# State space mixer: three kinds of loads on GpSimd's queue, the factors two quarters ahead

## The chip, the cores and the metric

The kernel runs on one core of a Trainium2 chip. The metric is the device time of one execution in microseconds; the numbers shown are the median of three runs. One execution was also recorded by the hardware profiler; all rows below come from it.

## What is computed

Two transformer blocks of two layers each on a sequence of 512 tokens and 1024 channels, all in float32. The change lies in the second block's second layer, the S5 state space mixer. Its core in the reference:

```python
u = h.reshape(b, seq, 64, 16)                 # 64 groups of 16 channels
mag = exp(lr * dt); ab = mag * (cos(li * dt) + i sin(li * dt))
bb = ((ab - 1) / (lr + i li))[..., None] * b  # 64 states to a group
bu = einsum('gpc,bsgc->bsgp', bb, u)
x = scan(x[t] = ab * x[t-1] + bu[t])          # over the sequence
y = real(einsum('gcp,bsgp->bsgc', c, x)) + d * u
g_a, g_b = split(gelu(y) @ w_glu, 2)
x_out = x_in + g_a * sigmoid(g_b)
```

(written here with complex numbers; the reference keeps real and imaginary parts apart).

## The kernel before

The sequence is cut into 64 steps of 8 tokens. A group then has a vector of 8 x 16 = 128 numbers at each of the 64 steps. Three things are made ahead, in the stage of the first feed-forward layer, and stored in the chip's HBM: `w_d`, the factors that turn 128 inputs into what one step adds to the states; `v_d`, the output factors that turn a state into 128 outputs; `k_d`, the kernels of the Toeplitz matrices, which map the 128 inputs of a step to outputs of the same step; and with them `tab_d`, the turns and decays by which the states are rotated and decayed from step to step.

`mixer3` works in four quarters of 16 groups. I call them 0 to 3. For each quarter q TensorE and VectorE do this:

- `blocks(q)`: 64 small products of the factors w and the inputs U[q] (line 1655), into PSUM.
- `states`: VectorE turns these by `tab` (lines 1671 to 1673), scans them with the decays (1674) and turns them back into X (1677 to 1681).
- `within(q)`: 32 products of U[q] and the Toeplitz matrices tm (line 1701).
- `outputs`: 64 products of X and the output factors v on top of them (line 1712); ScalarE copies the result out (1714).
- `gelus(q)`: eight transposes (1724), gelu on ScalarE, and a split into a high and a low part for the next projection (223, 224).

TensorE's order is written out by hand: blocks(0), within(0), blocks(1), outputs(0), then twice {within(q+1), blocks(q+2), gelus(q), outputs(q+1)}, then within(3), gelus(2), outputs(3) and the projection `w_gl`. All other engines' orders come from a planner, which lays the instructions out by their order in the program and by when it expects them to be ready; a load that needs a slot is placed with a wait for the last reader of the tile that was there.

The loads of the stage: the factors `w5` (1 MB a quarter) and turns `tab` (768 KB) by `s5_load` (lines 1611 to 1620), tm (1 MB, in eight pieces, line 1691) and v (1 MB, line 1693) by `factors`. Factors, tm and v share one tag, w5, with 4 slots; the profile names all three `w` and tells them apart by their source `w_d`, `k_d`, `v_d`. The turns have 2 slots. Factors and turns of quarters 0 and 1 are asked for through GpSimd's queue while the stage before (`ple(0)`, a gated projection with weights `w_pg`) still runs; those of quarters 2 and 3, all tm and all v go through SyncE's queue, each where the program comes to it: tm and v of q+1, then factors and turns of q+2. GpSimd has one computation in `mixer3`, the scaling of U[1] to U[3] (line 1736).

Of the kernel before, what the change touches and what calls it, by code (L numbers as in the profile page):

```python
# [140 lines left out]
def _build(ctx, tc, A, out, dbg, upto, cap):  # L141
    nc = tc.nc
    V, S, G, PE = nc.vector, nc.scalar, nc.gpsimd, nc.tensor

    def pool(stack, name, **kw):
        return stack.enter_context(tc.tile_pool(name=name, bufs=1, reuse_waits="tile", **kw))
# [7 lines left out]
    def tl(p, shape, tag, bufs=1, dt=F32):  # L154
        return p.tile(list(shape), dt, name=tag, tag=tag, bufs=bufs)
# [6 lines left out]
    def ps_(tag="ps", bufs=3):  # L162
        return tl(pp if tag in ("ps", "pm") else phase["px"], [128, T], tag, bufs)
# [1225 lines left out]
    w_d = tl(dp, [128, 32, 2, 128], "w_d")  # L1389
    v_d = tl(dp, [128, 32, 2, 128], "v_d")  # L1390
    tab_d = tl(dp, [128, 3, 32, 64], "tab_d")
# [218 lines left out]

    def s5_load(wq, q):

        if loaded:
            return loaded.pop(0)
        w = tl(wq, [128, 8, 2, 128], "w5", 4)
        e = nc.sync if q > 1 else G
        e.dma_start(w, w_d[:, 8 * q:8 * q + 8])
        tb = tl(wq, [128, 3, 8, 64], "tab", 2)
        e.dma_start(tb, tab_d[:, :, 8 * q:8 * q + 8])
        return w, tb  # L1620

    loaded = []

    def mixer3(U, wq, hp):
        with ExitStack() as st:
# [17 lines left out]
            def blocks(q):  # L1643

                if not q:
                    for h in range(2):
                        o = U[q].rearrange("p (b e) j -> p b e j", b=2)[:, :, 4 * h:4 * h + 4]
                        scaled.append(V.tensor_tensor(o, o, rj[:, None, None, :].to_broadcast([128, 2, 4, 64]), op=MUL).ins)
                w, tb = s5_load(wq, q)
                s = []  # L1650
                for a in range(2):
                    p = ps_("pb", 1) if a and q % 2 else ps_()
                    for e in range(8):
                        for ab in range(2):
                            PE.matmul(p[64 * ab:64 * ab + 64, e * 64:e * 64 + 64], w[:, e, a, 64 * ab:64 * ab + 64],
                                      U[q][:, 8 * ab + e], start=True, stop=True)
                    s.append(p)
                return s, tb

            def states(s, tb, gs=8):  # L1660

                tr, ti, rr = (tb[:, i].rearrange("p g j -> p (g j)") for i in range(3))
                X = tl(bp, [128, 2, 8, 64], "X", 2)
                V.memset(X[:, :, :, 0:1], 0.0)
                b = [tl(bp, [128, T], f"b{a}", 2) for a in range(2)]
                m = [f_() for a in range(2)]
                for g0 in range(0, 8, gs):
                    c, g = slice(g0 * 64, (g0 + gs) * 64), slice(g0, g0 + gs)
                    for a in range(2):
                        o, n = b[a][:, c], m[a][:, c]  # L1670
                        V.tensor_tensor(o, s[a][:, c], tr[:, c], op=MUL)
                        V.tensor_tensor(n, s[1 - a][:, c], ti[:, c], op=MUL)
                        V.tensor_tensor(o, o, n, op=SUB if a else ADD)
                        V.tensor_tensor_scan(o, rr[:, c], o, 0.0, op0=MUL, op1=ADD)
                    v = [y.rearrange("p (g j) -> p g j", g=8)[:, g, :63] for y in b + m]
                    for a in range(2):
                        V.tensor_tensor(X[:, a, g, 1:], v[a], tb[:, 0, g, :63], op=MUL)
                        V.tensor_tensor(v[2 + a], v[a], tb[:, 1, g, :63], op=MUL)
                    for a in range(2):
                        o = X[:, a, g, 1:]  # L1680
                        V.tensor_tensor(o, o, v[3 - a], op=ADD if a else SUB)
                return X
# [3 lines left out]
            def factors(q):  # L1686

                tm = tl(wq, [128, 16, 128], "w5", 4)
                for t in range(8):
                    o = 112 - 16 * t  # L1690
                    nc.sync.dma_start(tm[t:128:8], k_d[16 * q:16 * q + 16, :, o:o + 128].rearrange("g c m -> c g m"))
                v = tl(wq, [128, 8, 2, 128], "w5", 4)
                nc.sync.dma_start(v, v_d[:, 8 * q:8 * q + 8])
                return tm, v

            def within(q, tm):

                ps = [ps_("py", 2) for _ in range(2)]
                for e in range(8):
                    for ab in range(2):  # L1700
                        PE.matmul(ps[e // 4][sides[ab], e % 4 * 128:e % 4 * 128 + 128], U[q][:, 8 * ab + e], tm[:, 8 * ab + e],
                                  start=(e % 4 == 0), stop=False)
                return ps
# [14 lines left out]
            def gelus(q, o):  # L1718
                cs = (2 * q, 2 * q + 1)
                ys = [f_() for _ in cs]  # L1720
                for h in range(2):
                    p = ps_("pm", 2)
                    for t in range(4):
                        PE.transpose(p[:, t * 128:t * 128 + 128], o[:, 4 * h + t].rearrange("p e c -> p (e c)"), ident)
                    for ab, y in enumerate(ys):
                        S.activation(y[:, 256 * h:256 * h + 256].rearrange("p (t j) -> p t j", t=4),
                                     p.rearrange("p (t a j) -> p t a j", t=4, a=2)[:, :, ab], AF.Gelu_apprx_tanh)
                for c, y in zip(cs, ys):
                    if "s5" in dbg:
                        nc.sync.dma_start(dbg["s5"][c], y)  # L1730
                    acts.append(hl(hp, 8, y))

            s0 = blocks(0)
            with tc.issue_after(scaled[-1]):
                for q in range(1, 4):
                    G.tensor_tensor(U[q], U[q], rj[:, None, :].to_broadcast([128, 16, 64]), op=MUL)
            tm, v = factors(0)
            X = states(*s0, gs=4)
            y = within(0, tm)
            s1 = blocks(1)  # L1740
            o = outputs(y, v, X)
            X = states(*s1)
            for q in range(2):
                tm, v = factors(q + 1)
                y = within(q + 1, tm)
                s1 = blocks(q + 2)
                gelus(q, o)
                o = outputs(y, v, X)
                X = states(*s1)
            tm, v = factors(3)  # L1750
            y = within(3, tm)
            gelus(2, o)
# [328 lines left out]
    with ExitStack() as b2:  # L2081
# [8 lines left out]
        with ExitStack() as st:  # L2090
            p = pool(st, "s5u")
            wq = pool(st, "s5w")
# [32 lines left out]
```

## Time and profile before

| | |
|---|---|
| median of three runs | 2476.03 us (2470.3 to 2476.96) |
| profiled execution | 2467.97 us |
| its span | 2466.2 us |
| TensorE busy | 2339.5 us, 95% |
| VectorE busy | 1764.8 us, 72% |
| ScalarE busy | 1090.6 us, 44% |
| GpSimd busy | 518.4 us, 21% |

The span is the time from the first to the last instruction. Times in rows are microseconds from its start. The stage that the change touches lies between 1903 and 1965; the loads for it begin at 1855. In the rows PE is TensorE, DVE VectorE, ACT ScalarE, POOL GpSimd, SPq SyncE's queue.

### The profile page before, as it was taken

The page shows a single profiled execution, that of the slowest core. Times are in us where ns is not written, and L with a number is a line of the kernel's source. Part 1 is how long each engine was busy: PE and PEld are TensorE (multiplying, and loading weights), DVE is VectorE, ACT ScalarE, POOL GpSimd, SP SyncE. Part 2 cuts the span into 40 slices and gives each one's busy share as a digit, 9 for nine tenths or more (in the row PEclk, how much of TensorE's full clock was granted, in tenths as well). Part 3 has the DMA queues.
Part 4 walks back from the last instruction along what each step waited for, and adds up shares of the span by engine and source line. Part 5 has one row for each costly group of instructions (what it writes and reads, how often), then busy time and mean ns, then how long its engine had stood idle before and what let it go on. Part 6 is the DMA issues. An engine that isn't in the chain of part 4 may idle for free.

```text
span 2466.2 us, 35818 instructions
## 1 busy us (share of the span) xinstructions
PE 2339.5 (95%) x13205; PEld 1921.3 (78%) x13206; DVE 1764.8 (72%) x3319; ACT 1090.6 (44%) x1706; POOL 518.4 (21%) x510
## 2 busy tenths in 40 slices
PE   7999899899999998999989999999999899999999
PEld 4767799677777775899766777778787788888887
DVE  6985678699996886667686677737847756745755
ACT  3444588434443434786334434324433234433432
POOL 0001444100000002444110295666520000000000
PEclk9999899899999998999899999999999899999999
DMA  9862699554345222897421233344337632323342
GB/s 347 291 207 82 234 324 331 170 181 128 117 140 180 86 70 100 295 329 251 138 69 61 83 105 119 102 132 123 98 113 239 204 111 94 100 86 106 97 125 94
DMA packets 136790, 385.95 MB, mean 156 GB/s; under 512 B 24696, under 2 KB 41208, under 8 KB 134560
## 3 DMA queue, kind: packets, MB, share of 16 engines
q1 hardware_dynamic: 121408, 338.51, 41.5%
q0 software_dynamic: 7552, 26.74, 3.1%
q10 hardware_dynamic: 7648, 18.32, 2.1%
q8 instruction: 109, 1.79, 0.3%
q14 instruction: 73, 0.60, 0.1%
HBM read 354.13 MB, written 29.38 MB: 156 GB/s over the span
## 4 chain that ended last, share of the span: by engine, by line
PE 43%; DVE 7%; ACT 1%; issue 1%; DMA 0%; ACTq 0%; DVEq 0%
PE ps L268 13%; PE ps L270 13%; PE ps L269 13%; DVE wl L224 1%; DVE hc L2013 1%; ACT wh L223 0%; DMA tab<-tab_d 0%; PE pm L372 0%; PE sk L1587 0%; PE pa L512 0%; PE pm L530 0%; PE ps L1091 0%; PE ps L1092 0%; PE po L538 0%; DVE hc L2017 0%
## 5 line engine op out<-in xcount | busy, mean ns | idle before, releaser
L268 PE MATMUL ps<-hi,wh 128*128 128x512 f32 (+2 forms) x2248 | 898.9, 400 | 3.9 <-ACT hi L485 3.2
L270 PE MATMUL ps<-hi,wl 128*128 128x512 f32 (+2 forms) x2248 | 884.6, 394 | 8.8 <-DVE wl L224 8.8
L269 PE MATMUL ps<-lo,wh 128*128 128x512 f32 (+2 forms) x2248 | 884.5, 394 | 3.1 <-DVE lo L486 2.4
L223 ACT ACTIVATE wh<-w 128x1024 fp32r<-128x1024 f32 (+2 forms) x327 | 310.8, 951 | 572.1 <-PE ps L269 376.6
L224 DVE TENSOR_TENSOR wl<-w,wh 128x1024 fp32r<-128x1024 f32 (+3 forms) x323 | 371.3, 1150 | 211.6 <-ACT wh L223 207.3
L270 PEld LDWEIGHTS ps<-hi,wl 128*128 128x128 f32 (+1 forms) x2248 | 424.4, 189 | 109.2 <-DVE wl L224 13.8
L268 PEld LDWEIGHTS ps<-hi,wh 128*128 128x128 f32 (+1 forms) x2248 | 425.5, 189 | 106.7 <-issue 12.4
L269 PEld LDWEIGHTS ps<-lo,wh 128*128 128x128 f32 (+1 forms) x2248 | 425.2, 189 | 96.2 <-DVE lo L486 4.3
L224 DVE TENSOR_TENSOR wl<-we,wh 128x1024 fp32r<-128x1024 f32 x128 | 169.4, 1336 | 61.1 <-ACT wh L223 59.1
L929 POOL TENSOR_TENSOR hl<-hT,hh 128x1024 fp32r<-128x1024 f32 x60 | 138.4, 2307 | 173.3 <-ACT hh L928 96.0
L2013 DVE SCALAR_TENSOR_TENSOR hc<-f,cols,hc 128x511 f32<-128x511 f32 (+1 forms) x176 | 152.4, 866 | 6.4 <-ACT hc L2011 3.2
L223 ACT ACTIVATE wh<-we 128x1024 fp32r<-128x1024 f32 x128 | 135.3, 1059 | 47.6 <-PE pa L947 23.3
L909 PE MATMUL ps<-ht,w 128*128 128x128 f32 x1024 | 125.9, 276 | 5.2 <-ACT ht L959 5.0
L909 PEld LDWEIGHTS ps<-ht,w 128*128 128x128 f32 x1024 | 119.4, 192 | 7.4 <-ACT ht L959 7.1
L726 POOL IOTA io<- 128x512 f32 x2 | 1.1, 562 | 572.0 <-PE ps L270 415.6
L2009 DVE TENSOR_TENSOR f<-ps,rb 128x512 f32<-128x512 f32 x88 | 60.4, 686 | 71.2 <-PE ps L270 70.9
L441 DVE CUSTOM_DVE_ANT_0 we<-we,crow 128x1024 f32<-128x1024 f32 x80 | 96.3, 1214 | 3.4 <-DMA we<-in_ada_t_dram 3.1
L947 PE MATMUL pa<-wh,hh 128*128 128x256 f32 x496 | 89.2, 301 | 0.0
L223 ACT ACTIVATE hi<-hc 128x512 fp32r<-128x512 f32 x44 | 27.8, 632 | 128.0 <-DVE hc L2017 128.0
L491 DVE SCALAR_TENSOR_TENSOR x<-ps,mod,x 128x512 f32<-128x512 f32 x52 | 38.9, 748 | 59.0 <-PE ps L270 51.5
L947 PE MATMUL pa<-wl,hh 128*128 128x256 f32 x496 | 78.7, 281 | 1.4 <-DVE wl L224 1.4
L947 PE MATMUL pa<-wh,hl 128*128 128x256 f32 x496 | 79.1, 281 | 0.0
(572 smaller groups left out, 3319.1 us busy)
## 6 DMA issues: line engine op xcount, KB each, us to landing
we<-in_w_ex_dram SPq DMA_DIRECT2D x128, 512.0 KB, 5.7
w<-in_w_fu_dram SPq DMA_DIRECT2D x88, 512.0 KB, 3.5
we<-in_ada_t_dram SPq DMA_DIRECT2D x80, 512.0 KB, 5.0
w<-in_w_ex_dram SPq DMA_DIRECT2D x64, 512.0 KB, 5.4
w<-in_w_si_dram SPq DMA_DIRECT2D x48, 512.0 KB, 3.5
w<-in_w_fd_dram SPq DMA_DIRECT2D x32, 512.0 KB, 3.8
w<-in_w_ei_dram SPq DMA_DIRECT2D x20, 512.0 KB, 3.6
aw<-in_ada_w_dram SPq DMA_DIRECT2D x16, 512.0 KB, 10.2
```

The source lines that it names most:

```text
L223: S.activation(hi, src, AF.Copy)
L224: eng.tensor_tensor(lo, src, hi.bitcast(F32), op=SUB)
L268: PE.matmul(ps[:m], a, h, start=(not more and k + j == 0), stop=False)
L269: PE.matmul(ps[:m], a, l, start=False, stop=False)
L270: PE.matmul(ps[:m], b, h, start=False, stop=(last and k + j == nk - 1))
L441: V.tensor_tensor_reduce(w, w, row, 1.0, 0.0, op0=MUL, op1=ADD, accum_out=st[:, n:n + 1])
L491: V.scalar_tensor_tensor(xs[c], ps, mod(l, seg, c), xs[c], op0=MUL, op1=ADD)
L909: PE.matmul(p[:, c * 128:(c + 1) * 128], w2[:, (4 * q + c) * 128:(4 * q + c + 1) * 128], hd, start=True, stop=True)
L929: (V if e < 2 else G).tensor_tensor(hl_, win, hh.bitcast(F32), op=SUB)
L947: PE.matmul(hp[:, 0:256], h[:, 4 * n + k], w[:, k * 256:(k + 1) * 256], start=(n + i + k == 0), stop=(n + i + k == 6))
L2009: V.tensor_tensor(t, next(up)[1], rb, op=MUL)
L2013: V.scalar_tensor_tensor(c[:, d:], t[:, :T - d], C(f"fw{l}{2 - d}", n), c[:, d:], op0=MUL, op1=ADD)
```

## The change

The factors and turns of quarters 2 and 3, and all output factors, go through GpSimd's queue instead of SyncE's. The list `loaded`, in which the first two quarters' loads wait, is now filled in the loop too: factors and turns of q+2 are asked for in the program ahead of the Toeplitz matrices and output factors of q+1, and `blocks` takes them from the list.

```diff
     def s5_load(wq, q):
 
-        if loaded:
-            return loaded.pop(0)
         w = tl(wq, [128, 8, 2, 128], "w5", 4)
-        e = nc.sync if q > 1 else G
-        e.dma_start(w, w_d[:, 8 * q:8 * q + 8])
+        G.dma_start(w, w_d[:, 8 * q:8 * q + 8])
         tb = tl(wq, [128, 3, 8, 64], "tab", 2)
-        e.dma_start(tb, tab_d[:, :, 8 * q:8 * q + 8])
+        G.dma_start(tb, tab_d[:, :, 8 * q:8 * q + 8])
         return w, tb
...
-                w, tb = s5_load(wq, q)
+                w, tb = loaded.pop(0)
...
                 v = tl(wq, [128, 8, 2, 128], "w5", 4)
-                nc.sync.dma_start(v, v_d[:, 8 * q:8 * q + 8])
+                G.dma_start(v, v_d[:, 8 * q:8 * q + 8])
                 return tm, v
...
             for q in range(2):
+                loaded.append(s5_load(wq, q + 2))
                 tm, v = factors(q + 1)
                 y = within(q + 1, tm)
                 s1 = blocks(q + 2)
```

## Rows read from the trace of the kernel before

**Rows 1.** Busy time by stage: window, length, busy us (x instructions) of PE, PEld, DVE, ACT, POOL; clock, DMA share, GB/s
```profile
1903.00:1965.00 62.00, 44.90 (x675) 41.88 (x675) 52.03 (x101) 13.92 (x30) 7.91 (x3) 0.78 0.75 217
1965.00:2466.00 501.00, 496.07 (x2232) 410.84 (x2230) 294.75 (x392) 190.64 (x248) 0.00 (x0) 1.00 0.32 101
```

**Rows 2.** Timeline of TensorE, 1909 to 1966: start, us, line, what [idle before <-releaser]
```profile
1914.92 3.58 PE L1701 MATMUL py<-w,U 128*64 128x128 f32 x32
...
1929.70 3.06 PE L1701 MATMUL py<-w,U 128*64 128x128 f32 x32
1932.59 2.03 PE L1655 MATMUL ps<-U,w 128*64 128x64 f32 x64
...
1939.47 1.97 PE L1701 MATMUL py<-w,U 128*64 128x128 f32 x32 [0.19 <-ACT o L1714]
1944.65 1.20 PE L1655 MATMUL ps<-U,w 128*64 128x64 f32 x32 [3.21 <-DMA w<-w_d]
1945.61 1.96 PE L1655 MATMUL pb<-U,w 128*64 128x64 f32 x32
...
1949.25 3.71 PE L1712 MATMUL py<-w,X 64*64 64x128 f32 x64
...
1959.34 5.32 PE L1712 MATMUL py<-w,X 64*64 64x128 f32 x64 [2.69 <-DVE X L1681]
```

**Rows 3.** Timeline of VectorE, 1934 to 1961
```profile
1934.16 1.26 DVE L1681 TENSOR_TENSOR X<-X,f 128x504 f32<-128x504 f32 x2
...
1945.49 1.27 DVE L1681 TENSOR_TENSOR X<-X,f 128x504 f32<-128x504 f32 x2
1948.47 0.69 DVE L1671 TENSOR_TENSOR b<-ps,tab 128x512 f32<-128x512 f32 x1 [1.71 <-DMA tab<-tab_d]
```

**Rows 4.** The chain of waits, 1850 to 2010: start, us, what
```profile
1936.97 11.41 DMA tab<-tab_d
```

**Rows 5.** Timeline of SyncE's queue, 1840 to 2010
```profile
1915.18 6.08 SPq L1691 DMA_DIRECT2D w<-k_d  x8
...
1929.81 5.88 SPq L1691 DMA_DIRECT2D w<-k_d  x8
...
1936.42 0.38 SPq L1617 DMA_DIRECT2D w<-w_d  x1
...
1939.32 9.60 SPq L1691 DMA_DIRECT2D w<-k_d  x8
```

**Rows 6.** What SyncE's queue waited for, 1939 to 1950: us, times, longest
```profile
SPq L1691 <- DMA tab<-tab_d: 3.3, 1, 3.3
```

**Rows 7.** DMA issues: transfer, queue, count, size, median us to landing
```profile
v_d<-s_vr POOLq DMA_DIRECT2D x8, 256.0 KB, 2.8
...
w<-w_d POOLq DMA_DIRECT2D x2, 1024.0 KB, 8.7
...
tab<-tab_d POOLq DMA_DIRECT2D x2, 768.0 KB, 11.4
```

**Rows 8.** Line 1691, pieces of tm1, of tm2, of tm3 (each eight): us to landing
```profile
DMA to landing us min/median/max: 3.0/3.2/3.9
...
DMA to landing us min/median/max: 3.9/4.1/4.9
...
DMA to landing us min/median/max: 4.9/9.4/9.4
```

**Rows 9.** Timeline of GpSimd, 1780 to 2010
```profile
1908.87 7.91 POOL L1736 TENSOR_TENSOR U<-U,rj 128x1024 f32<-128x1024 f32 x3 [51.47 <-DVE rj L1639]
```

**Rows 10.** Timelines of VectorE and TensorE, the fourth column of the projection before
```profile
1872.59 1.23 DVE L224 TENSOR_TENSOR wl<-w,wh 128x1024 fp32r<-128x1024 f32 x1 [2.81 <-ACT wh L223]
...
1874.79 0.39 PE L270 MATMUL ps<-hi,wl 128*128 128x512 f32 x1
```

**Rows 11.** Busy time by stretch, columns as in rows 1
```profile
1940.00:1945.00 5.00, 1.79 (x38) 1.57 (x35) 5.00 (x9) 0.00 (x0) 0.00 (x0) 1.00 0.99 392
```

**Rows 12.** Line 1648: durations ns min/median/max, first and last start
```profile
L1648 DVE TENSOR_TENSOR U<-U,rj x2: 691/1761/2831, 1908.8 to 1909.4; 128x512 f32<-128x512 f32 x2
```

## The prediction

> **What bounds the kernel now.** The windows by stage come first [rows 1]. In the last 501 us, from 1965 on, TensorE is busy for 496.07; a microsecond won or lost before 1965 is therefore handed on to the end almost whole. In the 62 us of the state space stage (1903 to 1965) TensorE is busy for only 44.90 us, VectorE for 52.03. Of such a stretch the waits matter. The timeline of TensorE [rows 2] has two that bear on the change: 3.21 us before 1944.65, ended by the landing of the factors of quarter 3 (`w<-w_d`), and 2.69 us before 1959.34, ended by VectorE's X. VectorE's timeline [rows 3] shows why the first is not the dear one: states(2) ends at 1945.49 + 1.27 = 1946.76 and states(3) starts at 1948.47, after 1.71 us of waiting for `tab<-tab_d`, the turns of quarter 3. The chain of waits agrees: it runs through VectorE's states and has one transfer in it, those turns, 11.41 us from 1936.97 [rows 4]. What can be won here is thus those 1.71 us; TensorE's 3.21 us lie beside VectorE's states(2).
>
> **The change, part by part.** Nothing is computed more or less; eight transfers change their queue or their place (the four output factors, and factors and turns of quarters 2 and 3), and the four slots of tag w5 are handed out in another order. I number the quarters 0 to 3 and call the Toeplitz matrices tm.
>
> *SyncE's queue.* It loses the 2 x 2 factor and turn transfers and the 4 output factors. Today it asks for the factors of 3 at 1936.42, after tm2, whose eight pieces start at 1929.81 and take 5.88 us to ask for [rows 5]. It also pays later: of the eight pieces of tm3 the last ones wait, 3.3 us of it for the turns of 3 to land [rows 6]. These waits go, and the first weights of the next projection are asked for some microseconds sooner. Nobody late waits for either, so I price this at 0.
>
> *Factors of 3.* They go ahead of tm2 and so take the slot that tm2 takes today, the one free just before 1929.81 [rows 5]. Asked at about 1929.9, with 8.7 us to landing as GpSimd's earlier ones [rows 7], they are there by 1938.6. The wait of 3.21 us goes.
>
> *tm2.* It is late next. Its slot is now the one of tm1, which within(1) gives free: 1929.70 + 3.06 = 1932.76 [rows 2], 3 us after today. The last piece starts 5.88 - 0.6 = 5.3 us after the first, at 1938.1. How long a piece takes is bounded by 3.0 us (tm1 today, best) and 9.4 (tm3, behind 2.75 MB in the same queue) [rows 8]; tm2 has the queue to itself now, so I take 4.5, from tm2's own row of 3.9 to 4.9. Landed: 1942.6. Within(2) then starts at 1942.6 and not 1939.47. It took 1.97 us; after such an idle time TensorE ran blocks(3) in 1945.61 + 1.96 - 1944.65 = 2.92 where blocks(2), run without a pause, took 2.03 [rows 2], so I add 0.9: over at 1945.5. The first half of blocks(3) is ready at 1946.5, the second at 1947.5.
>
> *Turns of 3.* Both tab slots stay as they are; this one comes free with states(1), 1934.16 + 1.26 = 1935.42 [rows 3]. Asked at 1935.5 and not 1936.97, and no longer behind the factors and output factors of SyncE's queue. GpSimd's two turn transfers took 11.4 us (median), with 3.5 MB of their own queue around them; stores of GpSimd of a third of the size took 2.8 [rows 7]. Between 2.8 and 11.4 I take 8: 1943.5. At the upper end it is 1946.9, still within 0.2 us of the end of states(2). So states(3) starts with states(2)'s end, and its second operation meets the second half of blocks(3) at 1947.5 with some 0.1 us to wait: 1948.47 - 1946.87 = 1.6 us won. Outputs(3) follows X as today [rows 2, 3].
>
> *tm1 and the output factors of 1.* The factors of 2 take the first free slot; tm1 waits for within(0) to end, 1914.92 + 3.58 = 1918.5, 3.3 us later than 1915.18 [rows 2, 5]. 5.3 and 3.9 us later it has landed: 1927.7, for within(1) at 1929.70. Covered; with 9.4 us it would be 1933.2, and 3.5 us late, of which blocks(2) has 0.8 before VectorE feels it: the loss would be 2.7. The output factors of 1 may stand behind the turns of 2 in GpSimd's queue, which wait for states(0); outputs(1) wait for states(1) anyway, a whole quarter of VectorE's work later. Price 0. Of blocks(2)'s 0.8 us: it ends at 1932.59 + 2.03 = 1934.62 [rows 2], states(1) at 1935.42 [rows 3].
>
> *Output factors of 0.* They have no slot to wait for and GpSimd is idle for the 51.47 us before 1908.87, so from 1857.40 [rows 9], so I expect them at about 1857.4, 1 MB into the busiest stretch of loads. There one load of the projection before has little slack: its half for VectorE is done at 1872.59 + 1.23 = 1873.82 and first used at 1874.79, 1.0 us [rows 10]. At the pace of a full stretch, 392 GB/s [rows 11], 1 MB is 2.7 us; less the slack that bounds the loss by 1.7. The lower end is 0, below it nothing, since that load's queue loses nothing. I take 0.3: they stand last behind 3.5 MB of their own queue and meet that load only at its end. If GpSimd's queue puts them behind the scaling instead (1908.87 + 7.91 = 1916.8), 8.7 us make it 1925.5, and TensorE waits in outputs(0), in a stretch where VectorE has the pace; the 0.8 us of blocks(2) are left as cover there too.
>
> *The waits added to GpSimd's queue.* The scaling of U is its only computation there and stands ahead of them; nobody else waits behind a stuck transfer but the next transfer.
>
> Sum: 1.6 won, 0.3 lost, 1.3 us faster. The profiled execution took 2467.97 us (span 2466.2 and 1.8 around it) and would take 2466.7. It is 8.1 us below the median of the three timed runs, 2476.03, themselves 6.7 apart; the sum is a difference, so I put it on the median: 2474.7 us.
>
> **A rule against it.** In 1940 to 1945 the 16 DMA engines were busy to 0.99 and moved 392 GB/s [rows 11]: full, with all of it in one queue. The Trainium skill, "DMA: Bandwidth & Descriptors", section "Issuing engines are not separate DMA queues", says that transfers from several engines run on the same 16 DMA engines and that a second issuer saves only the time to issue. By the rows alone the sum above counts on order (factors of 3 some 6 us sooner), not on bandwidth; by that rule the turns of 3 would land no sooner than now and the sum would be 0, which is the first rival.
>
> **Rivals.**
> *No change* (0.22). The engines are full, the turns still land at 1948; or the freed SyncE lets the two splits of the next weights (0.68 us each) slip in among VectorE's states(3), +1.4 against 1.6. For it: the share of 0.99. Against: the factors of 3 move out of that stretch. 2476 us.
>
> *tm2 too late* (0.14), the slower side: 9.4 us for its last piece gives 1947.5, within(2) to 1950.4, blocks(3)'s first half at 1951.4, states(3) 3 us later than 1948.47: 2479 us. It decides from 1944.5 for tm2's landing, 2 us after my value. For it: the turns and output factors of GpSimd's queue run at the same time. Against: SyncE's queue holds nothing else.
>
> *GpSimd starved* (0.07). Row: VectorE's product of U took 2831 ns beside GpSimd's scaling, and 691 without [rows 12], so the two hold each other up. VectorE is busy all 5.00 us of 1940 to 1945 [rows 11]. If GpSimd could not put its transfers out until VectorE pauses, the turns of 2 would start at 1935.4 and those of 3 at the next pause; with 6 us to landing each (between the 2.8 and 8.7 of [rows 7]) that is 6 twice less the 1.7 waited for today, some 10 us: 2486. The Trainium skill, "SBUF — State Buffer", section "Who interferes with whom", has a lock of this kind, for some forms of VectorE's instructions. Against: GpSimd's stores landed in 2.8 us (median of eight) while VectorE worked [rows 7].
>
> *More is won* (0.12): outputs(3) took 5.32 us after the idle time, outputs(2), 64 of the same without a pause, 3.71 [rows 2]; with 1.6 us more won: 2473. Against: VectorE still ends last, so TensorE still waits before it.
>
> **How the numbers follow.** My case has 0.45. Within 0.3% (7.4 us, about what a measurement of this kernel can tell from no change) lie all but the starved queue; the runs' own spread moves a tenth of the cases over either bound, more below, as the profiled execution and one run lie well under the median. So 0.11 faster, 0.80 same, 0.09 slower. Range 2467 to 2482: from the winning case less the spread to tm2 too late and the spread. My own case: 2471 to 2478.
>
> **What would show it.** Right: no `tab` wait on VectorE near 1947, none on `w<-w_d` on TensorE, in its place a wait of some 3 us for `w<-k_d` ahead of within(2); GpSimd's first output factors near 1857. Wrong: states(3) starting after 1948.5, a TensorE gap in 1872 to 1876 above 0.5 us, or a GpSimd landing above 12 us.

## The result, and the profile after

The changed kernel takes 2506.71 us (median of six runs, 2496.67 to 2512.41); the kernel before, in the same session, 2476.49 us (2470.3 to 2481.23). The ratio is 1.0107, with a 95% interval of 1.0087 to 1.0127. Forecast were 2474.7 us, and a range that ended at 2482. The forecast was wrong, in sign and by 32 us.

The profiled execution of the changed kernel took 2496.67 us, of which 2494.9 are its span, 28.7 us more than the profiled execution before. The windows by stage of the kernel after (columns as in [rows 1]) say where:

```profile
1910.00:1993.40 83.40, 44.78 (x671) 42.26 (x672) 53.68 (x100) 13.76 (x30) 12.31 (x10) 0.73 0.56 149
1993.40:2494.90 501.50, 496.38 (x2232) 410.97 (x2232) 294.86 (x392) 191.04 (x248) 0.00 (x0) 1.00 0.33 101
```

After the stage nothing changed: 496.38 of 501.50 us busy on TensorE, 496.07 of 501.00 before. In the stage TensorE and VectorE work as long as before (44.78 and 53.68 us; 44.90 and 52.03), in a longer time, and the DMA engines moved 149 GB/s in place of 217. So it is waits. I measure the stage from here on from the product that makes rj (two matmuls into `pm`, just ahead of the scaling of U) to the end of outputs(3): 56.80 us before (1907.86 to 1964.66), 78.65 after (1914.70 to 1993.35), 21.85 more. Of the other 6.9 us, 6.1 stand ahead of the first instruction that was changed (GpSimd's ask for the factors of 0, at 1854.77 before and at 1860.83 after); in the other kernels below, whose work up to there is the same, it falls between 1858 and 1869, so I put this down to the spread between executions. 0.8 lie between that ask and the scaling of U.

The timeline of TensorE after has the waits. Line 1698 is within, 1652 blocks, 1709 outputs; line numbers from `states` on are three lower than before:

```profile
1934.58 3.57 PE L1709 MATMUL py<-w,X 64*64 64x128 f32 x32 [3.18 <-DVE X L1678]
1955.30 3.45 PE L1698 MATMUL py<-w,U 128*64 128x128 f32 x32 [17.15 <-DMA w<-k_d]
...
1971.27 3.68 PE L1698 MATMUL py<-w,U 128*64 128x128 f32 x32 [5.99 <-DMA w<-k_d]
...
1987.97 5.38 PE L1709 MATMUL py<-w,X 64*64 64x128 f32 x64 [3.28 <-DVE X L1678]
```

Within(1) waits for tm1 for 17.15 us; before, it followed at once at 1929.70 [rows 2]. Within(2) waits for tm2 for 5.99 us, before 0.19. The 3.21 us for the factors of 3 are gone, as forecast. VectorE's timeline shows that nothing covers the first wait any more:

```profile
1922.71 2.85 DVE L1670 TENSOR_TENSOR b<-b,f 128x256 f32<-128x256 f32 x1
...
1934.44 1.28 DVE L224 TENSOR_TENSOR wl<-w,wh 128x512 fp32r<-128x512 f32 x2
...
1959.72 0.69 DVE L1668 TENSOR_TENSOR b<-ps,tab 128x512 f32<-128x512 f32 x1 [14.57 <-PE ps L1652]
```

States(2) starts 14.57 us late, as blocks(2) stand behind within(1) in TensorE's order. The wait for `tab` of [rows 3] is gone. In the middle row are two splits of weights of the next projection. Why tm1 is late stands in SyncE's queue (timeline of its asks, after):

```profile
1915.06 20.42 SPq L241 DMA_DIRECT2D w<-in_w_gl_dram  x4
1935.58 9.46 SPq L1688 DMA_DIRECT2D w<-k_d  x8
...
1958.78 12.64 SPq L1688 DMA_DIRECT2D w<-k_d  x16
```

Before, the eight pieces of tm1 went out at 1915.18 [rows 5] and all weights of `w_gl` stood behind tm3, from 1949.66:

```profile
1949.66 56.75 SPq L241 DMA_DIRECT2D w<-in_w_gl_dram  x15
```

After, four weight loads stand ahead of tm1. Counted from the start of the stage, as the two traces are shifted against each other, the first weights are asked for at 0.36 us and not at 41.80, and tm1 at 20.88 and not at 7.32. What the queue waited for between 1930 and 1937 (us, times, longest):

```profile
SPq L241 <- DVE wl L224: 15.8, 1, 15.8
```

The fourth weight load needs a place that VectorE's split of an earlier one gives free. That split is the middle row above and stands behind states(0) in VectorE's order, at 1934.44, so the fourth load goes out at about 1935.2, and tm1, which has had its own place since 1924.9 (the end of within(0)), at 1935.58. It is a queue blocked by the load at its head.

Nor do the pieces land as before. Line 1688, the eight pieces of tm1, and the eight of tm2, us from ask to landing:

```profile
DMA to landing us min/median/max: 12.5/12.6/12.7
...
DMA to landing us min/median/max: 3.0/5.0/7.1
```

Tm1's pieces took 3.0 to 3.9 before [rows 8]. Tm2's late landing in this kernel is first of all a late ask: its slot is tm1's, and it goes out at 1958.78, when within(1) has ended. In 1935 to 1956 GpSimd's queue moved 3.67 MB (turns of 2, v1, factors and turns of 3) and held the engines for 55.1% of the time, SyncE's 1.57 MB and 35.8%. GpSimd's own timeline:

```profile
1863.45 0.56 POOL L1690 DMA_DIRECT2D w<-v_d  x1
1915.71 5.62 POOL L1733 TENSOR_TENSOR U<-U,rj 128x1024 f32<-128x1024 f32 x2 [51.70 <-DVE rj L1636]
1922.30 0.59 POOL L1614 DMA_DIRECT2D w<-w_d  x1 [0.97 <-PE ps L1652]
1922.90 2.36 POOL L1733 TENSOR_TENSOR U<-U,rj 128x1024 f32<-128x1024 f32 x1
...
1938.46 0.53 POOL L1614 DMA_DIRECT2D w<-w_d  x1 [2.94 <-PE py L1709]
1944.22 0.76 POOL L1616 DMA_DIRECT2D tab<-tab_d  x1 [5.23 <-DVE f L1675]
```

V0 is asked for at 1863.45, as early as forecast. The factors of 2 stand ahead of the third scaling of U and wait 0.97 us there for blocks(0), so that this scaling runs beside VectorE's product of 1922.71, which takes 2.85 us and not 1.21.

### The profile page after: what moved, and what is told of

Its sections match the earlier page's. It is cut to its first block, busy times and chain, and to the rows that moved or that the text cites. A ratio compares the mean times of both kernels' runs of the same rounds, so it can differ in the third digit from the quotient of the medians.

```text
span 2494.9 us, 35833 instructions
## 1 busy us (share of the span) xinstructions
PE 2342.3 (94%) x13205; PEld 1923.3 (77%) x13206; DVE 1768.5 (71%) x3319; ACT 1090.2 (44%) x1706; POOL 523.2 (21%) x518
```

## Experiments

Two theories. *Blocked queue*: the loss is made by what the planner put ahead of tm1 in SyncE's queue once that had been emptied. *Shared engines*: GpSimd's megabyte transfers and the Toeplitz pieces use the same 16 DMA engines, and the pieces land late wherever they stand in a queue. Two smaller suspects beside them: the order of factors of 2 and scaling, and v0's early transfer. The expectations name a third theory, *slots*: that the order in which the tag's four slots are handed out costs the time by itself. It wanted 2500 us or more in three kernels that took 2481 to 2485, and is out as the main cause. All runs in one table; each group has its own runs of the kernel before on the same chip (medians, in the order of the rows: 2476.49 for the changed kernel; 2476.18 for the next four; 2474.04 for four; 2476.74 for three; 2476.04 for the last two). The ratio is the one on record, and not the quotient of the two medians:

| kernel | us | ratio to before, 95% | stage, us | longest wait in it |
|---|---|---|---|---|
| before | 2476.49 | | 56.80 | 3.21 factors of 3 |
| changed | 2506.71 | 1.0107 (1.0087 to 1.0127) | 78.65 | 17.15 tm1 |
| weights behind tm3 | 2485.35 | 1.0039 (1.0023 to 1.0054) | 65.24 | 10.92 tm2 |
| changed order, old queues | 2481.33 | 1.0025 (1.0006 to 1.0044) | 62.60 | 9.56 tm1 |
| changed, v on SyncE | 2481.03 | 1.0019 (1.0000 to 1.0038) | 63.18 | 7.46 factors of 3 |
| all on GpSimd, old order | 2485.51 | 1.0030 (1.0011 to 1.0049) | 64.62 | 5.63 factors of 2 |
| weights behind, tm1 held | 2502.64 | 1.0104 (1.0081 to 1.0128) | 82.46 | 19.18 tm1 |
| weights behind, order, v0 on SyncE | 2480.74 | 1.0026 (1.0009 to 1.0043) | 62.23 | 7.78 tm2 |
| before, spare loads | 2485.73 | 1.0042 (1.0025 to 1.0059) | 65.45 | 5.53 factors of 3 |
| before, turns on GpSimd | 2472.77 | 0.9988 (0.9972 to 1.0005) | 54.49 | 2.03 tm2 |
| weights behind, order, v0 on SyncE, small loads | 2476.63 | 0.9997 (0.9980 to 1.0014) | 55.75 | 3.32 tm2 |
| before, v on GpSimd | 2482.04 | 1.0021 (1.0005 to 1.0037) | 58.55 | 4.13 tm2 |
| before, turns on GpSimd, again | 2476.01 | 0.9998 (0.9980 to 1.0017) | 53.80 | 2.02 tm3 |
| before, v0 on GpSimd | 2478.42 | 1.0007 (0.9991 to 1.0022) | 56.31 | 1.63 tm3 |
| changed, again | 2500.66 | 1.0103 (1.0082 to 1.0123) | 79.32 | 16.75 tm1 |

The last column is TensorE's longest wait for a load; waits of outputs for X come beside it.

The stage column holds one thing that is no wait. Outputs(3), its last piece of work, took 3.71 us in six versions, where the granted clock was 1.00 of full speed, and 5.05 to 5.38 in the others, where it was 0.68 to 0.72 (5.32 before; 6.59 at 0.55 with all on GpSimd). The six are old queues, spare loads, both with the turns, small loads, and v on GpSimd. So 1.6 us of a difference to before can be this clock. Why it fell in one and not in another stays open: these two (order and v0 on SyncE; the same with small loads) follow a wait of the same length.

```profile
1970.16 5.38 PE L1711 MATMUL py<-w,X 64*64 64x128 f32 x64 [3.27 <-DVE X L1678]
...
1970.51 3.71 PE L1713 MATMUL py<-w,X 64*64 64x128 f32 x64 [3.27 <-DVE X L1679]
```

Where it matters I give the stage up to the start of outputs(3) as well; before, that is 51.48 us.

**The weight loads put back behind tm3**, all else as changed.

```diff
+            last = [None]
...
-                    nc.sync.dma_start(tm[t:128:8], ...
+                    last[0] = nc.sync.dma_start(tm[t:128:8], ...
...
             early = []
-            for n in range(3):
+            with tc.issue_after(last[0].ins):
+              for n in range(3):
```

> The changed kernel, but the loads of the next projection's weights are kept behind the last piece of tm3 in SyncE's queue; all else as changed. Blocked queue (the fourth weight load waits 15.8 us for VectorE's split at the head of SyncE's queue, with tm1 behind it): without it tm1 is asked for when within(0) ends, lands before outputs(0) are over, and the wait of 17 us ahead of within(1) is gone; what is left is tm2, which waits for within(1)'s slot: 2474 to 2481, 20 us and more below the changed kernel. Shared engines (GpSimd's 1 MB transfers hold up the 512-byte packets of the Toeplitz pieces): pieces still take some 12 us to land, within(1) waits 5 us or more, 2482 to 2490. Slots (the order in which w5's slots are handed out is the cause): unchanged, 2500 or more.

Within(1) no longer waits; the stage is 13.4 us shorter and the kernel 2485.35 us. But within(2) now waits longer (TensorE; then the landing of tm2's pieces):

```profile
1939.83 1.97 PE L1700 MATMUL py<-w,U 128*64 128x128 f32 x32
...
1960.63 3.24 PE L1700 MATMUL py<-w,U 128*64 128x128 f32 x32 [10.92 <-DMA w<-k_d]
```

```profile
DMA to landing us min/median/max: 8.2/9.0/14.5
```

Tm2 is asked for from 1941.84 on, when within(1) has ended, and nothing stands ahead of it in its queue; its pieces took 3.9 to 4.9 us before. So the blocked queue is the larger part, 13.4 of the 21.9 us of the stage, and not all of it: the wait that went is the first theory's, the time lies where the second had it (2482 to 2490).

**Tm1 held, no weight load moved.** Is it the wait that costs, or the bytes of the weight loads ahead of tm1? The last kernel again, with tm1 held behind a copy of 512 bytes that waits for states(0):

```diff
+            scr = tl(dp, [128, 1], "scr")
+            held = nc.sync.dma_start(scr, X[:, 1, 7, 63:64]).ins   # X of states(0)
...
                 for t in range(8):
+                    with tc.issue_after(hold) if hold else nullcontext():   # hold: tm1 alone
                         last[0] = nc.sync.dma_start(tm[t:128:8], ...
```

> The version that keeps the weight loads behind the Toeplitz matrices (2485.35 us, stage from rj's matmul to the end of outputs(3) 65.24 us), with the eight loads of tm1 held in SyncE's queue behind a 512-byte copy that waits for the X of states(0). No weight load is moved, nothing else is moved. Blocked queue: the wait alone is what cost the changed kernel its 13.4 us above that version, so TensorE waits 9 to 17 us for k_d before within(1), the stage grows to 74 to 79 us and the time to 2495 to 2503 us. Rival, the bytes of the weight loads: without them ahead of tm1 the pieces land in 6 to 8 us, nearly all of the held time is hidden behind blocks(2) and states(1), and the time stays under 2489 us.

Its queue, and within(1) on TensorE:

```profile
1937.03 0.33 SPq L1741 DMA_DIRECT2D scr<-X  x1
1937.52 41.67 SPq L1692 DMA_DIRECT2D w<-k_d  x24
1979.30 1.48 SPq L242 DMA_DIRECT2D w<-in_w_gl_dram  x3
```

```profile
1960.09 3.68 PE L1702 MATMUL py<-w,U 128*64 128x128 f32 x32 [19.18 <-DMA w<-k_d]
```

No weights before 1979, the same wait, longer than expected (19.18 us for 9 to 17, and a stage of 82.46 for 74 to 79), and nearly the changed kernel's time: 2502.64. The wait in the queue is enough. Why 19.18 us, when the ask came some 10 us late? Of its eight pieces seven went out between 1937 and 1946, and they took 11.1 to 16.0 us to land. I read this as the second theory at work inside the first: an early ask hides a slow landing, a late one shows it.

**The same order on the old queues**, and **only v back on SyncE**: factors and turns two quarters ahead as changed; in the first all loads on the queues of before, in the second factors and turns on GpSimd's.

```diff
         w = tl(wq, [128, 8, 2, 128], "w5", 4)
-        G.dma_start(w, w_d[:, 8 * q:8 * q + 8])
+        e = nc.sync if q > 1 else G          # the first of the two only; turns likewise
+        e.dma_start(w, w_d[:, 8 * q:8 * q + 8])
...
-                G.dma_start(v, v_d[:, 8 * q:8 * q + 8])
+                nc.sync.dma_start(v, v_d[:, 8 * q:8 * q + 8])     # both
```

> The changed order in the program, all of it on the queues of the kernel before: factors and turns of q+2 ahead of tm and v of q+1, on SyncE's queue. Blocked queue: the turns of 2 now stand ahead of tm1 and wait for states(0); tm1 is asked for 10 us later than before and lands some 6 us after outputs(0) are over; the turns of 3 do the same to tm2: 2480 to 2488. Shared engines: no GpSimd transfer is added, so no slower than before, 2473 to 2478. Slots: as slow as the changed kernel, 2500 or more.

> The changed kernel with the output factors back on SyncE's queue; factors and turns stay ahead and on GpSimd's. In this build only three weight loads, for which buffers are free, stand ahead of tm1, and two more ahead of tm2. Blocked queue: nothing in front of tm1 waits long, so the 17 us are gone; the two ahead of tm2 wait for VectorE's splits behind states(0), about as long as tm2's own slot: 2475 to 2483. Shared engines: 3.5 MB still go through GpSimd's queue beside tm, 2482 to 2492. Slots: 2500 or more.

In the first the head of SyncE's queue is the turns of 2, which wait for states(0) as the weights did, with tm1 behind them:

```profile
1939.47 0.58 SPq L1617 DMA_DIRECT2D tab<-tab_d  x1
1940.15 5.56 SPq L1689 DMA_DIRECT2D w<-k_d  x8
```

Tm1 is late by the same mechanism with another load in the part, and within(1) waits 9.56 us. In the second the queue blocked is GpSimd's:

```profile
1933.31 0.76 POOL L1616 DMA_DIRECT2D tab<-tab_d  x1 [8.35 <-DVE f L1675]
1943.37 0.76 POOL L1616 DMA_DIRECT2D tab<-tab_d  x1 [9.30 <-DMA w<-k_d]
1944.12 0.55 POOL L1614 DMA_DIRECT2D w<-w_d  x1
```

The factors of 3 stand behind the turns of 3, and blocks(3) wait 7.46 us for them. Three weight loads stand ahead of tm1 here too, and cost nothing: they ask within 1.35 us, and the fourth is not among them. What counted here was whether the head of the queue waits, not how many loads are ahead.

**All on GpSimd, in the old order of the program.**

```diff
-        e = nc.sync if q > 1 else G
+        e = G
...
-                nc.sync.dma_start(v, v_d[:, 8 * q:8 * q + 8])
+                G.dma_start(v, v_d[:, 8 * q:8 * q + 8])
```

> The kernel before with factors, turns and output factors of all quarters on GpSimd's queue, in the old order of the program; no weight load stands ahead of a Toeplitz piece. Blocked queue: GpSimd's own queue holds the turns of 2 (waiting for states(0)) ahead of the output factors of 1 and the factors of 2, so blocks(2) come up to 4 us late, no more: 2475 to 2483. Shared engines: as in the changed kernel the tm pieces take 12 us to land, 2485 or more. Slots: the old order of slots, so 2473 to 2478.

No weights get ahead of tm1 here, and the kernel is 2485.51 us all the same. Blocks(2) wait for the factors of 2 (5.63 us), asked for at 1935.78 behind the turns of 2, which wait for states(0) until 1934.42. So a program order that is harmless on one queue blocks on another. The second theory has its part here too: the pieces of tm2 took 8.9 to 13.8 us, within(2) waited 2.56 us for them, and the time lies where that theory had it (2485 or more); tm1's took 3.1 to 4.2.

This version also tells something of why weights got ahead of tm1 in the changed kernel. SyncE's queue is just as empty here, and none did; but tm1 has its slot early, and its first piece goes out 7.3 us after the start of the stage, as before. In the changed kernel tm1 has to wait for within(0). So the empty queue alone is not enough; that it takes the late slot as well is my reading, and no run takes the planner's choice apart.

**The order mended and v0 back on SyncE**, on top of the weights put back.

```diff
-                    G.tensor_tensor(U[q], U[q], rj...
+                    scale3 = G.tensor_tensor(U[q], U[q], rj...
...
-                loaded.append(s5_load(wq, q + 2))
+                with tc.issue_after(scale3.ins):
+                    loaded.append(s5_load(wq, q + 2))
...
-                G.dma_start(v, v_d[:, 8 * q:8 * q + 8])
+                (G if q else nc.sync).dma_start(v, v_d[:, 8 * q:8 * q + 8])
```

> The version that keeps the weight loads behind the Toeplitz matrices (2485.35 us), with the load of w2 behind the third scaling of U in GpSimd's queue (so that the third scaling no longer stands beside VectorE's multiplications of states(0)) and v0 asked for by SyncE again. If these two are what is left beside the wait at within(2): the 2.85 us multiplication of VectorE goes back to about 1.2 (minus 1.6 us of the stage), the stretch from w0's ask to the first scaling of U goes from 57.2 back to 54 to 55 us, and the time is 2481 to 2483 us. Shared DMA engines: tm2's pieces still take 8 to 14 us to land beside GpSimd's megabyte loads, and TensorE still waits about 11 us for k_d before within(2). If the order of slots were the cause of that wait, it would fall below 4 us here, and the time to 2476.

VectorE, TensorE, and the landing of tm2's pieces:

```profile
1921.32 1.22 DVE L1670 TENSOR_TENSOR b<-b,f 128x256 f32<-128x256 f32 x1
```

```profile
1953.74 3.68 PE L1700 MATMUL py<-w,U 128*64 128x128 f32 x32 [7.78 <-DMA w<-k_d]
```

```profile
DMA to landing us min/median/max: 7.3/7.7/13.4
```

The product is back at 1.22 us, 1.6 won, and the stage is 3.0 us shorter. The wait for tm2 fell from 10.92 to 7.78 us, where some 11 had been expected, and stays far above the 4 us of the theory of slots. Is it that tm2 is asked for late (its slot is tm1's), or that it lands late?

**The same with small loads**: factors of 3 and output factors of 1 and 2 cut to an eighth, every order, slot and wait kept.

```diff
-        G.dma_start(w, w_d[:, 8 * q:8 * q + 8])
+        n = 1 if q > 2 else 8
+        G.dma_start(w[:, :n], w_d[:, 8 * q:8 * q + n])
...
+                n = 1 if q in (1, 2) else 8
+                (G if q else nc.sync).dma_start(v[:, :n], v_d[:, 8 * q:8 * q + n])
+                return tm, [v[:, e % n] for e in range(8)]
```

> The last version (order mended, v0 on SyncE: 2480.74 us, within(2) waiting 7.78 us for k_d) with GpSimd's loads of w3, v1 and v2 cut to an eighth, 128 KB for 1 MB, and the matmuls of blocks(3), outputs(1) and outputs(2) reading that eighth for every block; all orders, slots and waits stay. It leaves out seven eighths of those factors. Shared engines: the pieces of tm2 land in 3 to 6 us (7.5 there over the three quarters), the wait before within(2) falls to 1 to 4 us and the time to 2474 to 2478 us. Order of slots: tm2 is asked for just as late, the wait stays above 6 us and the time at 2479 to 2482 us.

TensorE at within(2), and the landing of tm2's pieces:

```profile
1953.12 3.68 PE L1702 MATMUL py<-w,U 128*64 128x128 f32 x32 [3.32 <-DMA w<-k_d]
```

```profile
DMA to landing us min/median/max: 2.8/3.2/7.7
```

The time is the time of before (0.9997). The stage is 6.5 us shorter than with whole loads (62.23 to 55.75); 4.8 of them come before outputs(3) starts, and are what the bytes on GpSimd's queue cost, nearly all of it at within(2) (7.78 to 3.32). The other 1.7 are outputs(3) at the higher clock. Up to outputs(3) the stage takes 52.04 us, 0.6 more than before. The 3.32 us that remain at within(2) come with the late slot; the prediction had some 3 for it.

**Spare loads beside the kernel before**: nothing moved (the weight loads of `w_gl` are tied to the place behind tm3 that they have in the kernel before; the lines below leave that out), and three loads of 1 MB into a tile that nothing reads, one behind the other from the end of states(0) on.

```diff
+            spare = tl(ap, [128, 2048], "spare")
+            G.tensor_copy(spare[:, 0:1], X0[:, 1, 7, 62:63])      # X0: X of states(0)
+            for i in range(3):
+                G.dma_start(spare.rearrange("p (g a c) -> p g a c", g=8, a=2), v_d[:, 8 * i:8 * i + 8])
             X = states(*s1)
```

> The kernel before, all its loads in their places, and three loads of 1 MB by GpSimd, one behind the other, into a spare tile that nothing reads, from the end of states(0) on: the sharing of the DMA engines by itself. Shared engines: the pieces of tm2 land in 7 to 13 us (3 to 5 before), within(2) waits 3 to 8 us for k_d, and the kernel takes 2479 to 2484 us. Rival (only orders and waits in queues count): the pieces land as before to within 2 us, and the time is within 0.1% of the kernel before (2474 to 2479).

The first spare load, TensorE at within(2) and blocks(3), and the landing of tm2's pieces:

```profile
1932.21 0.59 POOL L1748 DMA_DIRECT2D spare<-v_d  x1 [0.30 <-POOL spare L1746]
```

```profile
1949.42 1.97 PE L1703 MATMUL py<-w,U 128*64 128x128 f32 x32 [3.00 <-DMA w<-k_d]
1956.92 1.97 PE L1655 MATMUL ps<-U,w 128*64 128x64 f32 x32 [5.53 <-DMA w<-w_d]
```

```profile
DMA to landing us min/median/max: 9.4/10.0/10.5
```

The pieces of tm2 land in 10.0 us in place of 4.1, the turns of 3 come so late that VectorE waits 7.66 us for them, and the kernel takes 11.7 us more than its own runs of before, somewhat more than the 2479 to 2484 us expected of sharing. Sharing alone costs this, with every queue in its old order.

**Only v on GpSimd**, in the old order, and **only v0**.

```diff
-                nc.sync.dma_start(v, v_d[:, 8 * q:8 * q + 8])
+                G.dma_start(v, v_d[:, 8 * q:8 * q + 8])                        # the first
+                (nc.sync if q else G).dma_start(v, v_d[:, 8 * q:8 * q + 8])    # the second
```

> The kernel before with only the output factors v asked for by GpSimd, each at its old place in the program (w and the turns of 2 and 3 stay with SyncE, behind which the weight loads stay). Shared engines: a megabyte of v beside tm1 and beside tm2 slows their pieces to 6 to 9 us, TensorE waits 2 to 6 us for k_d before within(1) or within(2), and v0 at 1857 to 1870 us costs 0.4 to 2 us ahead of the stage: 2477 to 2481 us. Blocked queue alone: nothing is put ahead of a Toeplitz matrix, so the time is that of the kernel before, 2473 to 2477 us, less up to 1 us as tab2 and w3 no longer stand behind v in SyncE's queue.

> The kernel before with one transfer moved: the output factors of quarter 0 asked for by GpSimd, behind the turns of 1, and not by SyncE behind the first Toeplitz matrix. Price of v0 large: the stretch from the first ask of the factors to the scaling of U grows from 54.1 to 55 to 61 us, since the weights of the projection ahead of the stage land later (9.3 us median before, 13.8 in the version with all v on GpSimd), the stage stays at 56 to 58 us, and the time is 2478 to 2483 us. Price as predicted (0.3, at most 1.7): 2475 to 2478 us, and the stretch stays under 55.8.

The first: 4.13 us at within(2), and a stage 3.4 us longer up to outputs(3) and 1.8 with it, as it ran at the higher clock; in its profiled execution the rest is ahead of the stage. The second has that alone. GpSimd's timeline, and what ScalarE waited for in 1860 to 1920:

```profile
1861.87 0.57 POOL L1617 DMA_DIRECT2D w<-w_d  x1 [48.60 <-PE ps L270]
...
1922.83 7.93 POOL L1736 TENSOR_TENSOR U<-U,rj 128x1024 f32<-128x1024 f32 x3 [57.78 <-DVE rj L1639]
```

```profile
ACT wh L223 <- DMA w<-in_w_pg_dram: 9.0, 1, 9.0
```

From the first ask to the scaling 60.96 us, 54.10 before; the weights of the projection ahead of the stage are waited for 9.0 us on ScalarE, where it was 3.7, and TensorE stands for 3.3 of it. The other 3.5 us of the 6.9 are TensorE's clock: for the same 258 products it is busy 52.70 us at 0.91 of full speed, where it was 49.22 at 0.97 (the stretch from the first ask to the product of rj, v0 early and before, columns as in [rows 1]):

```profile
1861.87:1921.82 59.95, 52.70 (x258) 44.10 (x256) 40.93 (x80) 18.86 (x28) 3.18 (x5) 0.91 0.70 225
...
1854.77:1907.86 53.09, 49.22 (x258) 42.22 (x256) 40.66 (x80) 18.88 (x28) 2.63 (x4) 0.97 0.74 234
```

Over all profiles with v0 early that stretch was 54.40, 54.88, 56.15, 57.15, 58.97, 60.67 and 60.96 us; over the eight with v0 late 54.01 to 54.77. So v0 early costs between nothing and 6.9 us, from one kernel and execution to another. In the timed runs of this kernel it is 2.4 us, which can't be told from nothing (0.9991 to 1.0022).

**Only the turns on GpSimd**, and the factors ahead of the output factors in SyncE's queue; weights kept behind tm3. Run twice.

```diff
-        e.dma_start(tb, tab_d[:, :, 8 * q:8 * q + 8])
+        G.dma_start(tb, tab_d[:, :, 8 * q:8 * q + 8])
...
+                if 0 < q < 3:
+                    got.append(s5_load(wq, q + 1))
                 v = tl(wq, [128, 8, 2, 128], "w5", 4)
```

> The kernel before with only the turns of quarters 2 and 3 asked for by GpSimd (each when its slot comes free, nothing behind them in that queue), the factors one place ahead of the output factors in SyncE's queue, and the weight loads of the next projection kept behind tm3. Blocked queue: no wait for tab ahead of a Toeplitz piece or ahead of weights, the 1.71 us of VectorE's wait for tab goes, the 3.21 us wait for w_d falls to 1 to 3 us, and the time is 2473 to 2476 us, not to be told from the kernel before. Shared engines alone: 768 KB beside tm2 and tm3 slow their pieces from 3 to 5 us to 6 to 9, TensorE waits 2 to 5 us for k_d, and the time is 2477 to 2480 us.

> The version with only the turns on GpSimd's queue once more on another chip, since its ratio of 0.9988 left open whether it is faster: with the 2.3 us that its stage was shorter by in the trace, 0.9985 to 0.9995 and an interval that holds 1 or ends just under it. If the 2.3 us were chance, the ratio is 0.9995 to 1.0015.

The stage is 2.3 and 3.0 us shorter in the two profiles; 1.6 us of each are outputs(3) at the higher clock, and 0.7 and 1.4 are won up to its start. VectorE's wait for `tab` is 0.76 us in the first and none in the second. In time the kernel is 1.3 and 0.7 us under the kernel before, both intervals hold 1, and the second ratio, 0.9998, lies where chance had been put: no version here is shown to be faster. TensorE in the first of the two:

```profile
1946.30 3.53 PE L1705 MATMUL py<-w,U 128*64 128x128 f32 x32 [2.03 <-DMA w<-k_d]
1950.78 1.15 PE L1655 MATMUL ps<-U,w 128*64 128x64 f32 x32 [0.94 <-DMA w<-w_d]
```

**The changed kernel again**, to see whether the 8 us between the medians (30.2) and the stage (21.9) have a place.

> The changed kernel as it is, once more on the chip of the run beside it. If the 8 us outside the stage are v0's, the stretch ahead of the stage is 56 to 61 us in this profile and the time is 2500 to 2510 us; if the first profiled execution was a quick one, the stretch is 54.5 to 55.5 again and the stage is longer than 78.65 us, 80 to 88. In both cases tm1 is asked for behind four weight loads, after states(0).

Neither of the two. The stretch ahead of the stage was 54.40 us and the stage 79.32, both as in the first profile; the median was 24.6 us over its runs of before. The queue and the waits are the same (the profile puts the first of them down to a weight load of the same queue):

```profile
1911.57 20.66 SPq L241 DMA_DIRECT2D w<-in_w_gl_dram  x4
```

```profile
1951.54 3.68 PE L1698 MATMUL py<-w,U 128*64 128x128 f32 x32 [16.75 <-DMA w<-in_w_gl_dram]
...
1968.97 3.68 PE L1698 MATMUL py<-w,U 128*64 128x128 f32 x32 [7.04 <-DMA w<-k_d]
```

The 22.5 us of the second stage leave 2 us of the second median, and the two losses of medians differ by 5.6. But the ratios agree, 1.0107 and 1.0103, that is some 26 us, and the low ends of their intervals (21.5 and 20.3 us) reach down to the stage's 21.9 and below its 22.5. So it is not shown that anything outside the stage is lost.

## Why the prediction was wrong

**The step that failed** is SyncE's queue: "the first weights of the next projection are asked for some microseconds sooner. Nobody late waits for either, so I price this at 0." Counted from the start of the stage, they were asked for 41.4 us sooner (41.80 to 0.36), ahead of tm1, and the fourth of them waited for VectorE with tm1 behind it. Two kernels price it: taking it out of the changed one gives 13.4 us of the stage back, and putting its wait alone in again takes 17.2. The part asked who waits for the weights; it should have asked what else would then stand ahead of tm1, and what the new head of the queue waits for. The trace of before has rows for that: fifteen weight loads behind tm3 in the same queue, and what they wait for (SyncE's queue, 1949 to 2010: us, times, longest):

```profile
SPq L241 <- DVE wl L224: 45.1, 12, 6.7
```

That the planner would put them ahead of tm1 no row of before shows. The rival *No change* had half of it, the splits of the next weights among VectorE's work; what it did not have is that the loads themselves would stand in the queue.

**Mis-sized: tm2's landing.** "tm2 has the queue to itself now, so I take 4.5". The queue it had to itself, the engines not. With the weights out of the way its pieces took 8.2 to 14.5 us and within(2) waited 10.92 us in place of 3; with small loads beside them 2.8 to 7.7 and 3.32. The slot and the order of that step were right, and 4.5 us of the wait (7.78 to 3.32) are the bytes beside it. The rival *tm2 too late*, at 0.14, had the mechanism ("the turns and output factors of GpSimd's queue run at the same time") and a price of 3 us for up to 9.4 us of landing. The argument set against it ("SyncE's queue holds nothing else") was the same mistake of queue for engine.

**The rule weighed against the change** said this, and was applied to the turns alone. The Trainium skill, "DMA: Bandwidth & Descriptors", section "Issuing engines are not separate DMA queues", has transfers from all issuers interleave on the same 16 engines. The spare loads agree: 4.1 us to land became 10.0. By that rule the sum was set to 0; for the Toeplitz pieces it means a loss, which these runs priced.

**Tm1** was to be asked for when within(0) ends, and to be covered. That held where nothing blocked its queue: in the version with the weights behind, tm1's pieces went out from 1926.7 on, and within(1) had no wait. They took 6.1 to 7.7 us to land where 3.9 had been forecast, and the cover was long enough for that.

**The waits in GpSimd's queue**: "the scaling of U ... stands ahead of them". Two of three scalings did. The third behind the factors of 2 cost VectorE 2.85 - 1.22 = 1.6 us. And "nobody else waits behind a stuck transfer but the next transfer" held in words, while that next transfer was what blocks(2) or blocks(3) waited for in two of the versions (5.63 and 7.46 us).

**Output factors of 0**: at 1863.45, early as forecast. 0.3 us was the price, 1.7 the bound; the bound was too tight: six of seven profiles show more than 0.3 and five more than 1.7, the highest 6.9. What was compared was 1 MB at full pace against one load's slack; what happened is that the weight loads beside it landed in 13.7 us (median) and not 9.3, and that TensorE's clock was lower after the wait. The sign "a GpSimd landing above 12 us" could not tell: v0 took 20.2 us in the changed kernel's second profile, but the turns of 1 took 13.9 in the kernel before.

**Factors of 3, turns of 3**: neither the 3.21 us nor the 1.71 us wait is left in the kernel after, as forecast. That is no proof of the landings, as tm1 and tm2 made all of quarter 3 late there. The times to landing were about right: in the changed kernel's second profile 9.6 us (8.7 forecast) and 9.5 (8 forecast; its upper end of 11.4 was the median of two, of which one had taken 13.9). The 1.6 us that they should have won are not shown. Up to outputs(3) the stage is 0.6 us longer with small loads, and 0.7 and 1.4 shorter with the turns alone. What makes those three stages 1.1, 2.3 and 3.0 us shorter is mostly what the rival *More is won* named: outputs(3) in 3.71 us and not 5.32. It did not take a shorter wait ahead of it (3.27 us with small loads, 2.69 before).

**After the stage**: "a microsecond won or lost before 1965 is therefore handed on to the end almost whole". It was: 501.50 us after it against 501.00.

The rival *GpSimd starved* is not borne out: in the kernel after, GpSimd's turns of 3 went out at 1944.22, with states(1) (its end 1945.1) still running on VectorE, and they waited for their slot, not for a pause of VectorE.

## What to carry to other kernels

A load taken off a queue makes room, and something may move up into it; list what that may be, and what each of those loads waits for, before pricing the gap at nothing. A queue's worth is its order: the head that waits sets the time of all behind it, however few bytes they have. A second queue added asks here and not engines: small pieces on the critical path paid for large transfers beside them (4.1 us to land became 10.0), so leave the large ones where they stood behind the pieces, or early enough that their landing does not meet them.

## What the runs showed of the hardware

Pieces of 128 KB in rows of 512 bytes landed in 3 to 5 us with little beside them, and mostly in 7 to 16 us with megabyte transfers of another queue under way (10.0 with one at a time, in the kernel with spare loads). Beside the 768 KB of turns alone, tm2's median was 8.2 us in one profile and 4.0 in the other of the same kernel, so single profiles don't price such an overlap. The DMA engines are then busy and slow: of 1935 to 1956 in the kernel after, this is the slices' busy share in tenths and GB/s,

```profile
DMA  0898998989999999999999999999989999973000
GB/s 0 148 335 203 265 312 187 261 300 359 430 416 429 370 219 338 383 364 414 352 299 189 181 192 193 209 220 207 227 185 304 339 356 312 230 160 119 23 0 0
```

with slices of nine tenths at 430 GB/s and others, as busy, at 181. So a busy share near 1 tells that the engines are held, not how many bytes pass. In this window SyncE's 1.57 MB, two thirds of them Toeplitz pieces, held the engines 1.5 times as long for each byte as GpSimd's 3.67 MB (35.8% and 55.1% of the time). And a transfer that was asked for 50 us ahead of its use, into a stretch that the profile shows as full (v0), moved the end of that stretch by up to 6.9 us, half of it a wait and half the lower clock that TensorE had in that stretch (0.91 for 0.97).
